# A hybrid mLSTM and attention trunk in split float32: stacked score operands, first loads in another order, a last block in two banks, new order lists

## The chip, the core and the metric

The kernel runs on one core of one Trainium2 chip. The metric is the device time of one execution in microseconds (us). The kernel before was run three times: 927.72, 929.80 and 930.09 us, median 929.80 us. One further execution was profiled.

## What is computed

An encoder trunk of two layers on 256 tokens of width 1024, all in float32. Each layer has a SwiGLU block, a mixer and another SwiGLU block, each followed by a layer norm of the scaled input plus the block's output. The mixer of layer 0 is a bidirectional chunkwise mLSTM with 4 heads, that of layer 1 is windowed attention with 16 query heads, 4 key heads, an ALiBi distance term and a sink logit.

```python
def reference(x, ...):
    for l in range(DEPTH):                                  # 2 layers
        x = layer_norm(ALPHA * x + 0.5 * swiglu(x, ffn_w_in[l, 0], ffn_w_out[l, 0]), ln_g[l, 0], ln_b[l, 0])
        j = l // N_MIXERS
        if l % N_MIXERS == 0:
            y = mlstm_mixer(x, ml_w_in[j], ml_gate_b[j], ml_norm_g[j], ml_w_out[j])
        else:
            y = window_attention(x, at_w_in[j], at_sink[j], at_w_out[j])
        x = layer_norm(ALPHA * x + y, ln_g[l, 1], ln_b[l, 1])
        x = layer_norm(ALPHA * x + 0.5 * swiglu(x, ffn_w_in[l, 1], ffn_w_out[l, 1]), ln_g[l, 2], ln_b[l, 2])
    return x

def swiglu(x, w_in, w_out):                                 # 1024 -> 2 * 2816 -> 1024
    gu = x @ w_in
    return (jax.nn.silu(gu[..., :D_FF]) * gu[..., D_FF:]) @ w_out

# window_attention, the scores of one head (HEAD_DIM = 64)
s = q @ k.T * HEAD_DIM ** -0.5 - slope * dist               # where |t - s| <= 128, else -1e30
m = max(max(s), sink); pe = exp(s - m)
attn = pe / (sum(pe) + exp(sink - m)); o = attn @ v

# mlstm_chunkwise weights all pairs of tokens by running maxima of the gates
```

## The kernel before, in words

**Split operands.** TensorE multiplies in its rounded float32 form (fp32r). To keep float32 accuracy every operand is held as two parts, a high one (`_hi`, the rounded value) and a low one (`_lo`, the rest). One exact product is three matmuls into one PSUM bank: high by high, high by low, low by high (`mm3`). The two parts are made by ScalarE (ACT: the cast that gives the high part) and VectorE (DVE: the subtraction that gives the low part); `split_evac` does both for a PSUM bank.

**Weights.** All weights are streamed from memory in pieces of 512 KB. A piece lands in a raw buffer (`w_raw`, 4 of them, and `s_raw`, 8 more in the SwiGLU stages), ACT writes its `w_hi`, DVE its `w_lo` (each a ring of ten places), and TensorE (PE) uses both. There are 412 such splits. The SwiGLU stages compute part of their first product by a seven-product scheme (`seven`), which adds raw pieces to each other (on DVE, or in the transfer itself on the POOL queue) and multiplies by sums `S1` to `S4` of the transposed input `xT`. `down` adds the second product into four banks that stay open through the stage. `b_mm` is the first block of a SwiGLU stage.

**Start.** The four halves of `x` are fetched on ACT's queue and weight pieces on SP's. PE warms up on transposes of the identity (`warm`), transposes `x` in halves (`to_xT`), and begins with the first weight piece.

**mLSTM.** The running maxima of both directions are in 64 rows. Their high and low parts are two tiles `pn_hir` and `pn_lor` of 128 rows, the rest zero. `weights(h)` spreads one row over 128 partitions by a matmul with a column of the negated identity `neg_id`, once for each part.

**Attention.** Two query heads stand one above the other in 128 rows of `q_hir` and `q_lor` (64 rows each). The keys are in `kp_hir` and `kp_lor`, twice, once in the upper 64 rows with zeros below and once below zeros, so that one matmul of 512 columns gives the scores of both heads (2 x 256 keys). `scores(j)` runs for a pair of heads j (0 to 7) and two token blocks: three such matmuls and one more with `neg_id` that subtracts the distances `dist`. Then follow the maximum (`rm`, DVE), the exponential (`sc`, ACT), the division (`scale`, POOL), eight transposes (`turn`), their split (`pr`), the product with the values (`values`) and the sum of its parts into `q_hir` and `q_lor` of that pair, whose queries are no longer needed. Projections still due (`q_rest`) and output products (`out_proj`) stand between the steps.

**Last norm.** `tail` finishes the four output blocks one after the other; `Norm` takes the statistics of each 512 columns (`half`), then mean, spread, and two passes (`finish`). The result goes out in four transfers.

**Order.** Every instruction is first recorded (`Program`) and then issued in the order of a list of numbers, `ORDER`; another table, `SLOTS`, gives the place of each tile in its ring. Both are written out in the file. Each engine runs its own instructions strictly in that order. Since all operations pass through one recording helper, all have its line in the profile (L301): they are told apart by the names of their tiles.

## Time and profile before

| | |
|---|---|
| median of three runs | 929.80 us (927.72 to 930.09) |
| the profiled execution | 931.54 us, its span 929.8 us |
| mean granted TensorE clock | 0.997 |
| busy: PE, weight loads, DVE, ACT, POOL | 98%, 82%, 87%, 62%, 16% of the span |
| matmuls | 4368 |
| memory read | 206.65 MB |

The profiled execution lasted 1.7 us longer than its span, and 1.7 us longer than the median of the three others. In the profile a matmul is listed with the time from its start to its modelled end. Matmuls overlap, so the time that one costs is the distance between the starts of two that follow each other. `PEld` is the loading of the stationary operand, which overlaps PE. SPq and POOLq are the transfers that SP and POOL start.

### The profile page before, as it was taken

Reading aid. Unit: us, or ns where it says so; the run is one execution under the profiler, and the core shown is the slowest. Engines: PE = TensorE matmul, PEld = TensorE weight load, DVE = VectorE, ACT = ScalarE, POOL = GpSimd, SP = SyncE. Lnnn points to the kernel's source line nnn. Section 1 sums busy time; section 2 is a strip of 40 time slices with the busy share of each in tenths; the row PEclk is TensorE's granted clock in tenths of the full one; section 3 lists DMA queues with packets and bytes.
Section 4 is the critical chain, followed back from the end, with each engine's and each line's share of the span. In section 5 each row is a group of like instructions: output and inputs, shape, how many; then the busy total and the mean of one; then the engine's idle time right before and its main releaser. Section 6 shows DMA issues by size and latency. Waiting matters only on the chain.

```text
span 929.8 us, 12210 instructions
## 1 busy us (share of the span) xinstructions
PE 912.3 (98%) x4368; PEld 758.3 (82%) x4368; DVE 809.7 (87%) x955; ACT 578.5 (62%) x814; POOL 148.1 (16%) x202
## 2 busy tenths in 40 slices
PE   9999999999999999999999999999999999999996
PEld 7887888889988888888888888888887788888875
DVE  6999789887688999879899997998888799987985
ACT  7766477454764667566647674764678568656650
POOL 0331111010110111112012111112335211202100
PEclk9999999999999999999999999999999999999998
DMA  9999799566283889797968988985732378898751
GB/s 339 301 302 263 248 269 226 182 195 218 87 300 109 248 247 246 245 294 206 302 225 206 272 254 242 289 208 185 250 133 68 136 232 252 218 327 212 231 159 45
DMA packets 100637, 208.50 MB, mean 224 GB/s; under 512 B 6848, under 2 KB 21200, under 8 KB 100576
## 3 DMA queue, kind: packets, MB, share of 16 engines
q1 hardware_dynamic: 82368, 173.04, 52.8%
q0 software_dynamic: 17632, 33.64, 21.4%
q10 hardware_dynamic: 576, 1.05, 0.3%
q8 instruction: 34, 0.56, 0.2%
q14 instruction: 27, 0.22, 0.1%
HBM read 206.65 MB, written 1.05 MB: 223 GB/s over the span
## 4 chain that ended last, share of the span: by engine, by line
PE 78%; DVE 7%; DMA 5%; issue 4%; ACT 4%; POOL 0%; SPq 0%; POOLq 0%; ACTq 0%; DVEq 0%
PE p L301 78%; DVE w_lo L301 4%; DMA s_raw<-in_ffn_w_in_dram 3%; ACT w_hi L301 2%; DMA w_raw<-in_ffn_w_out_dram 1%; DVE s_raw L301 1%; DMA w_raw<-in_ffn_w_in_dram 1%; DVE t L301 0%; ACT wt L301 0%; DMA x<-in_x_dram 0%; SPq L301 0%; DVE x L301 0%; DVE pr_lor L301 0%; ACT t L301 0%; DVE rm L301 0%
## 5 line engine op out<-in xcount | busy, mean ns | idle before, releaser
L301 ACT CAST w_hi<-s_raw 128x1024 fp32r<-128x1024 f32 x234 | 240.4, 1051 | 128.8 <-DMA s_raw<-in_ffn_w_in_dram 36.6
L301 DVE TENSOR_TENSOR w_lo<-s_raw,w_hi 128x1024 fp32r<-128x1024 f32 x234 | 278.5, 1218 | 28.7 <-ACT w_hi L301 28.5
L301 DVE TENSOR_TENSOR w_lo<-w_raw,w_hi 128x1024 fp32r<-128x1024 f32 (+1 forms) x171 | 205.2, 1215 | 29.2 <-ACT w_hi L301 28.8
L301 ACT CAST w_hi<-w_raw 128x1024 fp32r<-128x1024 f32 (+1 forms) x171 | 176.9, 1046 | 80.4 <-PE p L301 42.9
L301 PE MATMUL p<-w_hi,xT_hi 128*128 128x512 f32 x512 | 204.3, 399 | 0.0
L301 PE MATMUL p<-w_lo,xT_hi 128*128 128x512 f32 x512 | 199.7, 390 | 1.1 <-DVE w_lo L301 1.1
L301 PE MATMUL p<-w_hi,xT_lo 128*128 128x512 f32 x512 | 200.1, 391 | 0.0
L301 PE MATMUL p<-w_hi,h_hir 128*128 128x512 f32 x320 | 125.6, 393 | 0.0
L301 PE MATMUL p<-w_lo,h_hir 128*128 128x512 f32 x320 | 124.7, 390 | 0.8 <-DVE w_lo L301 0.8
L301 PE MATMUL p<-w_hi,h_lor 128*128 128x512 f32 x320 | 124.9, 390 | 0.4 <-DVE h_lor L301 0.4
L301 PEld LDWEIGHTS p<-w_hi,xT_lo 128*128 128x128 f32 x512 | 96.3, 188 | 20.8
L301 PEld LDWEIGHTS p<-w_lo,xT_hi 128*128 128x128 f32 x512 | 96.5, 188 | 19.9 <-DVE w_lo L301 1.4
L301 PEld LDWEIGHTS p<-w_hi,xT_hi 128*128 128x128 f32 x512 | 96.5, 188 | 19.0 <-ACT w_hi L301 0.4
L301 POOL DMA_DIRECT2D s_raw<-in_ffn_w_in_dram x42 | 51.1, 1218 | 330.1 <-DVE w_raw L301 87.7
L301 PE MATMUL p<-w_hi,S_hir 128*128 128x512 f32 x256 | 100.0, 391 | 1.1 <-ACT t L301 1.1
L301 PE MATMUL p<-w_lo,S_hir 128*128 128x512 f32 x256 | 99.8, 390 | 0.7 <-DVE w_lo L301 0.7
L301 PE MATMUL p<-w_hi,S_lor 128*128 128x512 f32 x256 | 99.7, 389 | 0.0
L301 PEld LDWEIGHTS p<-w_hi,h_lor 128*128 128x128 f32 x320 | 60.1, 188 | 13.7 <-DVE h_lor L301 1.1
L301 PEld LDWEIGHTS p<-w_lo,h_hir 128*128 128x128 f32 x320 | 60.1, 188 | 13.4 <-DVE w_lo L301 1.2
L301 PEld LDWEIGHTS p<-w_hi,h_hir 128*128 128x128 f32 x320 | 60.1, 188 | 12.0
L301 PEld LDWEIGHTS p<-w_hi,S_hir 128*128 128x128 f32 x256 | 48.1, 188 | 12.1 <-ACT t L301 2.2
L301 PEld LDWEIGHTS p<-w_lo,S_hir 128*128 128x128 f32 x256 | 48.1, 188 | 11.0 <-DVE w_lo L301 1.1
(201 smaller groups left out, 1204.6 us busy)
## 6 DMA issues: line engine op xcount, KB each, us to landing
s_raw<-in_ffn_w_in_dram SPq DMA_DIRECT2D x104, 512.0 KB, 6.6
w_raw<-in_ffn_w_in_dram SPq DMA_DIRECT2D x56, 512.0 KB, 5.8
s_raw<-in_ffn_w_out_dram SPq DMA_DIRECT2D x54, 512.0 KB, 6.6
s_raw<-in_ffn_w_in_dram POOLq DMA_DIRECT2D x42, 512.0 KB, 6.7
w_raw<-in_ffn_w_out_dram SPq DMA_DIRECT2D x34, 512.0 KB, 7.1
w_raw<-in_ml_w_in_dram SPq DMA_DIRECT2D x24, 512.0 KB, 4.7
w_raw<-in_ffn_w_in_dram POOLq DMA_DIRECT2D x22, 512.0 KB, 7.6
w_raw<-in_at_w_in_dram SPq DMA_DIRECT2D x12, 512.0 KB, 4.0
```

The source lines that it names most:

```text
L301: f(*args, **kw)
```

## The change

- **Scores from stacked parts.** For each head the high part of the query (64 rows) stands over its low part (64 rows) in one tile `q2r`, and the keys stand twice in `kk_hir` and in `kk_lor`. One matmul of 256 columns with `kk_hir` then adds high by high and low by high, and one with `kk_lor` the other two products. A pair of heads takes four matmuls of 256 columns in place of three of 512. The distance matmul of 512 columns stays and comes first. The queries are split in 64-row pieces (`stacked`), twice as many as before; the keys in 128-row pieces, half as many; the zeroing of `kp` and `pn` on POOL goes.
- **Maxima stacked.** High and low part of the running maxima stand in one tile `pnr`; one matmul with `neg_two`, which has -1 in two rows, replaces two.
- **First loads.** The halves of `x` go on SP's queue among the first weight pieces, the first piece in two transfers, the second piece is split in halves too. The second warm-up has 6 transposes instead of 10. The transposes of the second token block come after that block's first need, those of the second half of the columns one weight piece later.
- **Last columns in two banks.** The last three weight pieces of the last output block are multiplied in two halves of 256 columns, the second half into a bank of its own, and statistics are taken in three parts.
- **Lists anew.** `ORDER` and all of `SLOTS` are new, and attention has two raw buffers more. The new order lets matmuls of several products take turns on PE, where the old one had them mostly in blocks.

```diff
@@ -35,248 +35,267 @@
-WHOLE = 21792
+WHOLE = 21728
...
-    "0 1 1 1 2 35 -34 63 -61 1 75 -74 1 89 -88 1 1 1 1 1 1 156 -155 1 1 22 -19 1 -3 4 1 93 -92 13 -18 6 1 -26 27 "
...
+    "10 -10 9 2 -10 12 1 -12 13 1 -13 14 1 -14 15 1 -15 16 1 -16 17 -16 17 1 -17 18 3 1 1 4 84 -87 1 -6 7 2 116 "
...
@@ -378,7 +397,10 @@
             t = t.rearrange("p (k f) -> p k f", k=w["k"])
-            if isinstance(w["src"], list):
+            if i == 0:
+                for k in range(2):
+                    self.nc.sync.dma_start(t[:, k], w["src"][:, k])
+            elif isinstance(w["src"], list):
                 for k, src in enumerate(w["src"]):
@@ -390,7 +412,7 @@
         lo = self.rooms.take("w_lo", [128, D], FR)
-        if i == 0:
+        if i < 2:
             for j in range(2):
...
@@ -563,16 +583,22 @@
         s_ = slice(h * 512, h * 512 + 512)
-        nc.scalar.dma_start(xt[t][:, s_], x[0, t * 128:(t + 1) * 128, s_])
+        nc.sync.dma_start(xt[t][:, s_], x[0, t * 128:(t + 1) * 128, s_])
 
     xT = (state.tile([128, 8, S], FR, name="xT_hi", tag="xT_hi"),
           state.tile([128, 8, S], FR, name="xT_lo", tag="xT_lo"))
+    for name, n in (("stats", 18), ("mv", 2), ("rs", 2)):
+        rooms.kind(name, tiles(name, n, F32, 2))
 
     W = Weights(nc, rooms, words, plan, after)
     load_x(0, 0)
+    W.load(plan[0]["word"])
     load_x(1, 0)
+    W.load(plan[1]["word"])
     load_x(0, 1)
     load_x(1, 1)
+    W.load(plan[2]["word"])
+    W.load(plan[3]["word"])
     nc.scalar.preload_act_table(AF.Silu)
@@ -600,6 +627,7 @@
         nc.vector.tensor_scalar(neg_id, ident, -1.0, None, op0=OP.mult)
+        nc.vector.scalar_tensor_tensor(neg_two, ident[:, 0:64], -1.0, ident[:, 64:128], op0=OP.mult, op1=OP.subtract)
 
@@ -656,7 +684,15 @@
             self.t, self.ca, self.eps, self.gb, self.last = t, ca, eps, gb, last
-            self.stats = rooms.take("stats", [128, 2, 6], F32)
+            self.stats = rooms.take("stats", [128, 3 if last and t else 2, 6], F32)
+
+        def add(self, c, y, ca=None):
+            z = xt[self.t][:, c:c + 256]
+            nc.vector.scalar_tensor_tensor(z, z, ca or self.ca, y, op0=OP.mult, op1=OP.add)
+
+        def piece(self, i, c, y, ca=None):
+            self.add(c, y, ca)
+            nc.vector.bn_stats(self.stats[:, i], xt[self.t][:, c:c + 256])
 
@@ -685,14 +721,26 @@
                 final = t == 1 and o == 1
+                own = len(todo[t]) - 3 if last and final else None
                 for n, (c, w) in enumerate(todo[t]):
                     if between is not None and t == 0 and o == 1 and n == turn_at:
                         between()
                     if final and n == turn_at:
                         emit_x(0, last)
-                    mm3(y[t][o], h(c, t), pair(w, A, 0, slice(o * 512, o * 512 + 512)),
-                        first and n == 0, n == len(todo[t]) - 1)
-                norm[t].half(o, y[t][o])
+                    if own is not None and n >= own:
+                        mm3(y[t][o][:, 0:256], h(c, t), pair(w, A, 0, slice(512, 768)), False, n == len(todo[t]) - 1)
+                    else:
+                        mm3(y[t][o], h(c, t), pair(w, A, 0, slice(o * 512, o * 512 + 512)),
+                            first and n == 0, n == len(todo[t]) - 1)
+                if own is None:
+                    norm[t].half(o, y[t][o])
+                else:
+                    z = ybank()
+                    norm[t].piece(1, 512, y[t][o][:, 0:256])
+                    norm[t].add(768, y[t][o][:, 256:512])
+                    for n, (c, w) in enumerate(todo[t][own:]):
+                        mm3(z[:, 0:256], h(c, t), pair(w, A, 0, slice(768, 1024)), n == 0, n == 2)
+                    norm[t].piece(2, 768, z[:, 0:256], 1.0)
             norm[t].finish()
@@ -716,8 +764,7 @@
                 to_xT(0, xt[0], ybank, (0,))
-                warm(10)
-                to_xT(1, xt[1], ybank, (0,))
+                warm(6)
             hs, pieces = [], []
@@ -781,10 +828,12 @@
                     for a in range(4):
-                        if m == 0 and a == 1:
+                        if m == 0 and a == 2:
                             for t in range(2):
                                 to_xT(t, xt[t], ybank, (1,))
                         for t in range(2):
+                            if m == a == 0 and t:
+                                to_xT(1, xt[1], ybank, (0,))
                             b_mm(ps[t], t, m, a)
@@ -955,9 +1004,7 @@
                     nc.gpsimd.memset(p[:, :, 256:258].bitcast(F32), one)
-            pn = both([128, S], "pn")
-            for p in pn:
-                nc.gpsimd.memset(p.bitcast(F32), 0.0)
+            pn = tile_([128, S], FR, "pn")
             ones = tile_([64, 1], F32, "ones")
@@ -1006,9 +1053,7 @@
                 nc.vector.tensor_tensor_scan(pm[q, ord_], ones[q].to_broadcast([32, S]), u[q, ord_], 0.0, op0=OP.mult, op1=OP.max)
-            dst = pair(pn, slice(0, 64))
-            nc.scalar.copy(dst[0], pm)
-            nc.vector.tensor_sub(dst[1], pm, dst[0].bitcast(F32))
+            split_evac((pn[0:64], pn[64:128]), pm)
             ex = fe
@@ -1035,9 +1080,7 @@
                     r = 32 * d + h
-                    sel = neg_id[:, r:r + 1].to_broadcast([128, 128])
-                    nc.tensor.matmul(pb[:, d], sel, pn[0], start=True, stop=False)
-                    nc.tensor.matmul(pb[:, d], sel, pn[1], start=False, stop=True)
+                    nc.tensor.matmul(pb[:, d], neg_two[:, r:r + 1].to_broadcast([128, 128]), pn, start=True, stop=True)
                 for sb in range(2):
@@ -1202,9 +1245,7 @@
                 nc.gpsimd.memset(qs_col[64 * (h % 2):64 * (h % 2) + 64, h // 2:h // 2 + 1], 0.125 / slope[8 + h])
-            kp = both([128, 4, 2, S], "kp")
-            for p in kp:
-                nc.gpsimd.memset(p.bitcast(F32), 0.0)
+            kk = both([128, 4, S], "kk")
             fwd = tile_([128, 2, S], F32, "fwd", tag="sc", bufs=6)
@@ -1218,7 +1259,8 @@
             va = [tile_([128, 4, 2, 64], FR, f"v{t}") for t in range(2)]
-            qT = both([128, 8, S], "q")
+            q2 = tile_([128, 8, 2, S], FR, "q2")
+            rooms.kind(f"raw.{keys[bound[0]]}", raws + pool.new("s_raw", D, 2, F32))
             kd, qd = [], []
@@ -1248,15 +1290,19 @@
                     nc.tensor.transpose(p[:, g], kd[t][:, g].rearrange("p a d -> p (a d)"), ident)
-                for a in range(2):
-                    r = slice(64 * a, 64 * a + 64)
-                    split_evac(pair(kp, r, A, a, tok(t)), p[r])
+                split_evac(pair(kk, A, A, tok(t)), p)
+
+            def stacked(j, a, m, src, scale=None):
+
+                r = slice(64 * a, 64 * a + 64)
+                split_evac((q2[0:64, j, a, m], q2[64:128, j, a, m]), src[r], scale[r] if scale is not None else None)
 
             def q_turn(t):
                 p = ybank((128, 4, 128))
                 for j in range(4):
                     nc.tensor.transpose(p[:, j], qd[t][:, j], ident)
-                split_evac(pair(qT, A, slice(0, 4), tok(t)), p)
+                for a in range(2):
+                    stacked(slice(0, 4), a, tok(t), p)
 
@@ -1268,7 +1314,8 @@
                     if k == 7:
-                        split_evac(pair(qT, A, 4 + 2 * g + f), p, qs_col[:, 2 * g + f:2 * g + f + 1])
+                        for a in range(2):
+                            stacked(4 + 2 * g + f, a, A, p, qs_col[:, 2 * g + f:2 * g + f + 1])
                         if f == 1:
@@ -1296,8 +1343,10 @@
                     p = ps[t]
-                    mm3(p, pair(qT, A, j, tok(t)), pair(kp, A, g), True, False)
-                    nc.tensor.matmul(p, neg_id, dist[:, t, None, :].to_broadcast([128, 2, S]), start=False, stop=True)
+                    nc.tensor.matmul(p, neg_id, dist[:, t, None, :].to_broadcast([128, 2, S]), start=True, stop=False)
+                    for a in range(2):
+                        for e in range(2):
+                            nc.tensor.matmul(p[:, a], q2[:, j, a, tok(t)], kk[e][:, g], start=False, stop=a == e == 1)
                     nc.vector.reduce_max(rm[:, t], p, axis=AX.X)
@@ -1391,7 +1440,7 @@
                     o = sums.pop(st - 3)
-                    d = pair(qT, A, st - 3)
+                    d = q2[:, st - 3, 0], q2[:, st - 3, 1]
                     nc.scalar.copy(d[0], o)
@@ -1404,7 +1453,7 @@
             todo = [(c, wo[c]) for c in range(8)]
-            return tail(y, lambda c, t: pair(qT, A, c, tok(t)), (todo[7:], [todo[c] for c in range(8) if c not in CT]), False, norm, last, 4)
+            return tail(y, lambda c, t: (q2[:, c, 0, tok(t)], q2[:, c, 1, tok(t)]), (todo[7:], [todo[c] for c in range(8) if c not in CT]), False, norm, last, 4)
 
```

What the list does to the order is seen in the instructions as they stand on an engine. In the rows below a number behind a name is a buffer.

On PE, in the first SwiGLU stage, the first of the seven products: `S_hir` and `S_lor` are the parts of `S1`, `xT` those of the input, `h` those of the activations for `down`, `p` is a PSUM bank. Before:

```order
L301 MATMUL p_95<-w_hi_71,S_hir_0_159 128x512
L301 MATMUL p_95<-w_lo_81,S_hir_0_159 128x512
L301 MATMUL p_95<-w_hi_71,S_lor_0_160 128x512
L301 MATMUL p_95<-w_hi_71,S_hir_0_159 128x512
L301 MATMUL p_95<-w_lo_81,S_hir_0_159 128x512
L301 MATMUL p_95<-w_hi_71,S_lor_0_160 128x512
L301 MATMUL p_95<-w_hi_73,S_hir_0_159 128x512
L301 MATMUL p_95<-w_lo_82,S_hir_0_159 128x512
L301 MATMUL p_95<-w_hi_73,S_lor_0_160 128x512
```

The same place after:

```order
L320 MATMUL p_91<-w_hi_75,xT_hi 128x512
L320 MATMUL p_92<-w_hi_70,S_hir_0_160 128x512
L320 MATMUL p_92<-w_lo_86,S_hir_0_160 128x512
L320 MATMUL p_91<-w_lo_83,xT_hi 128x512
L320 MATMUL p_94<-w_hi_76,h_hir_1_99 128x512
L320 MATMUL p_91<-w_hi_75,xT_lo 128x512
L320 MATMUL p_92<-w_hi_70,S_lor_0_161 128x512
L320 MATMUL p_94<-w_lo_80,h_hir_1_99 128x512
L320 MATMUL p_91<-w_hi_75,xT_hi 128x512
L320 MATMUL p_92<-w_hi_77,S_hir_0_160 128x512
```

The block of one product has become three products in turn, each with its own pieces of weights.

On PE, in attention, the scores of one token block and what follows them. Before:

```order
L301 MATMUL p_88<-kp_hir_0_230,q_hir_0_241 128x512
L301 MATMUL p_88<-kp_lor_0_231,q_hir_0_241 128x512
L301 MATMUL p_88<-kp_hir_0_230,q_lor_0_242 128x512
L301 MATMUL p_88<-distr_0_238,neg_id 128x512
L301 MATMUL p_94<-xT_hi,w_hi_74 128x256
L301 MATMUL p_94<-xT_lo,w_hi_74 128x256
L301 MATMUL p_94<-xT_hi,w_lo_84 128x256
```

After, the two token blocks of a pair of heads (`p_91` and `p_95`):

```order
L320 MATMUL p_91<-distr_0_238,neg_id 128x512
L320 MATMUL p_94<-xT_lo,w_hi_68 128x256
L320 MATMUL p_91<-kk_hir_0_230,q2r_0_241 128x256
L320 MATMUL p_91<-kk_lor_0_231,q2r_0_241 128x256
L320 MATMUL p_95<-kk_hir_0_230,q2r_0_241 128x256
L320 MATMUL p_91<-kk_hir_0_230,q2r_0_241 128x256
L320 MATMUL p_94<-xT_hi,w_lo_82 128x256
L320 MATMUL p_91<-kk_lor_0_231,q2r_0_241 128x256
```

Each block has five matmuls instead of four, four of them of half the length, and those of the other block and of a projection (`p_94`) stand between them.

On ACT, at the very start. Before:

```order
L301 CAST w_hi_68<-w_raw_64 128x512
L301 CAST xT_hi<-p_89 128x4x128
L301 CAST w_hi_68<-w_raw_64 128x512
L301 ACT_TABLE_LOAD
L301 CAST xT_hi<-p_91 128x4x128
L301 CAST w_hi_69<-w_raw_65 128x1024
```

After:

```order
L320 CAST w_hi_73<-w_raw_64 128x512
L320 CAST xT_hi<-p_95 128x4x128
L320 CAST w_hi_73<-w_raw_64 128x512
L320 CAST w_hi_71<-w_raw_65 128x512 x2
L320 CAST xT_hi<-p_90 128x4x128
L320 CAST w_hi_75<-w_raw_67 128x1024
```

The cast of the second token block's transposed input (`xT_hi<-p_91` before, `xT_hi<-p_90` after) now stands behind both halves of the second weight piece, and the four transfers that ACT issued ahead of all this are gone.

91 lines of the change are left out of this document (45 added, 46 removed), and 397 rows, old and new, of the table ORDER.

## The prediction

> **What bounds the kernel now.** I read the page first, for the engines and the chain.
>
> ```profile
> PE 912.3 (98%) x4368; PEld 758.3 (82%) x4368; DVE 809.7 (87%) x955; ACT 578.5 (62%) x814; POOL 148.1 (16%) x202
> ...
> PE 78%; DVE 7%; DMA 5%; issue 4%; ACT 4%; POOL 0%; SPq 0%; POOLq 0%; ACTq 0%; DVEq 0%
> ```
>
> PE is busy for 912.3 of 929.8 us and carries 78% of the chain that ends last. So PE work that goes away counts almost in full, and so does every wait on PE. DVE, with 87%, is the only other engine that can become the bound. Next I read the waits of PE.
>
> ```profile
> PE p L301 <- DVE w_lo L301: 2.6, 3, 1.1
> PE p L301 <- DVE ident L301: 1.5, 1, 1.5
> PE p L301 <- ACT t L301: 1.1, 2, 0.7
> PE p L301 <- DMA x<-in_x_dram: 0.7, 1, 0.7
> PE p L301 <- ACT q_hir L301: 0.7, 2, 0.4
> PE p L301 <- ACT kp_hir L301: 0.6, 1, 0.6
> PE p L301 <- DVE pr_lor L301: 0.5, 1, 0.5
> PE p L301 <- ACT sc L301: 0.4, 1, 0.4
> PE p L301 <- DVE h_lor L301: 0.4, 1, 0.4
> PE p L301 <- DVE a_lor L301: 0.3, 1, 0.3
> PE p L301 <- POOL sc L301: 0.2, 1, 0.2
> PE p L301 <- DVE kp_lor L301: 0.2, 1, 0.2
> ```
>
> The columns are the time in total, the number of waits and the longest. Without `ident` and `x`, which belong to the start, there are 14 waits that sum to 7.0 us. Seven are attention's (`q_hir`, `kp`, `pr`, `sc`; 2.6 us), three are for weights. The rest of the time PE runs at the pace of its matmuls. That pace, and what a wait costs, I took from the timeline of PE.
>
> ```profile
> 641.01 0.39 PE L301 MATMUL p<-w_lo,h_hir 128*128 128x512 f32 x1
> ...
> 648.04 0.39 PE L301 MATMUL p<-w_hi,h_lor 128*128 128x512 f32 x1
> ```
>
> The first column is the start in us. Between these two rows lie 31 steps of matmuls of 512 columns, so one costs 7.03 / 31 = 0.227 us. The PSUM bank changes after every third of them, and the step does not.
>
> ```profile
> 214.25 0.28 PE L301 MATMUL p<-xT_lo,w_hi 128*128 128x256 f32 x1
> ...
> 219.76 0.28 PE L301 MATMUL p<-xT_hi,w_lo 128*128 128x256 f32 x1
> 219.88 0.28 PE L301 MATMUL p<-pn_hir,neg_id 128*128 128x256 f32 x1
> ...
> 220.33 0.28 PE L301 MATMUL p<-xT_hi,w_hi 128*128 128x256 f32 x1
> ```
>
> From the first to the second row are 46 steps: 0.120 us for 256 columns, a little more than half of 0.227. The four matmuls with `pn` take 0.45 / 4 = 0.113 us each.
>
> ```profile
> 897.57 0.39 PE L301 MATMUL p<-w_hi,S_lor 128*128 128x512 f32 x1
> 898.66 0.50 PE L301 MATMUL p<-w_hi,S_hir 128*128 128x512 f32 x1 [0.71 <-ACT t L301]
> ```
>
> Here a wait of 0.71 us made a step of 1.09 instead of 0.227: it cost 0.86, 0.15 more than it lasted. With that the 14 waits cost 7.0 + 14 x 0.15 = 9.1 us.
>
> **The change part by part.** All sums are made against the profiled execution (931.54 us, span 929.8) and carried over to the median of the three runs, 929.8, as differences.
>
> *Scores.* Eight pairs of heads by two token blocks make 16 blocks. In each, three matmuls of 512 (0.680) become four of 256 (0.480): 0.20 saved, 16 x 0.20 = 3.2 us, all on PE. The saving hangs on the short matmul keeping its 0.120. 46 in a row keep it. The Trainium skill, TensorE: Matmul & The Clock Gate, section Back-to-back issue gap, has another rule: in a sustained stream a matmul takes about 131 ns at 512 columns and 81 at 128. On a straight line between these an estimate for 256 columns is 98 ns, three of 131 cost what four of 98 do, and the term would be 0, the sum of all parts 5.6 us instead of 8.8. The rows above, 227 and 120 ns, disagree with it.
>
> The price is on ACT and DVE: the queries' split takes twice the instructions at half the rows, and an instruction costs by its columns. The two more of 512 columns are given back by the keys; four more of 256 are left on either engine, at 0.42 (worked out with the last block below) 1.7 us, spread over the projections. DVE has 13% free, so I cost it at nothing; uncovered it would be 1.7 us. POOL loses the zeroing of the keys, off every path.
>
> *Maxima.* Eight matmuls at 0.113 go: 0.9 us. `neg_two` is one small DVE instruction more, early, bounded by 0.2.
>
> *Last block.* Nine matmuls of 512 become 18 of 256: 9 x (0.240 - 0.227) = +0.12 us.
>
> ```profile
> 921.31 0.39 PE L301 MATMUL p<-w_hi,h_lor 128*128 128x512 f32 x1
> 921.74 0.69 DVE L301 SCALAR_TENSOR_TENSOR x<-x,p 128x512 f32<-128x512 f32 x1 [0.89 <-PE p L301]
> 922.46 0.69 DVE L301 BATCH_NORM_STATS2 stats<-x 128x6 f32<-128x512 f32 x1
> ```
>
> After the last matmul DVE needs the sum and the statistics of 512 columns, 2 x 0.72 = 1.44 us. For 256 columns I take 0.42 (half would be 0.35, the bounds are 0.35 and 0.69). In the 1.08 us of the last nine matmuls DVE gets through the first 256 columns' sum and statistics and the other sum, 1.3 us, so it is 0.2 to 0.3 late; then 0.42 twice: 1.1 us. Saved 0.32, with PE's 0.12 net 0.2 (0 to 0.5).
>
> *Start.*
>
> ```profile
> 2.00:3.00 1.00, 1.00 (x6) 1.00 (x5) 0.00 (x0) 0.24 (x1) 0.00 (x0) 1.00 0.61 190
> 3.00:4.00 1.00, 0.85 (x4) 0.45 (x3) 0.00 (x0) 1.00 (x1) 0.00 (x0) 1.00 0.92 313
> ```
>
> ```profile
> 4.54 1.12 PE L301 MATMUL p<-ident,x 128*128 128x128 f32 x4 [0.70 <-DMA x<-in_x_dram]
> 5.45 0.62 ACT L301 CAST w_hi<-w_raw 128x512 fp32r<-128x512 f32 x1 [1.41 <-DMA w_raw<-in_ffn_w_in_dram]
> ...
> 8.30 0.78 PE L301 MATMUL p<-w_hi,xT_hi 128*128 128x512 f32 x1
> ...
> 9.72 0.41 PE L301 MATMUL p<-w_hi,xT_hi 128*128 128x512 f32 x1
> ...
> 12.59 0.47 PE L301 MATMUL p<-w_hi,xT_hi 128*128 128x512 f32 x1
> ```
>
> In the first view the last column is GB/s. Before, `x` shares the transfers with the first piece and lands at 4.5; PE begins the first piece at 8.30 and the second at 12.59, with all transposes done; so two pieces are done at 12.59 + 12 x 0.227, with the slow first step 15.4. After, the first half of `x` is alone in front. Its 0.26 MB are through at about 3.2 by the rates above, and I take 3.7 for its landing. Six warm-up transposes and the casts put the first matmul at about 5.9, and the halves of the first `w_lo` hold its six to 7.7; transposes of the second block to 8.1. Then comes the new wait: on ACT the cast of this block's `xT_hi` is queued behind two half casts of the second piece. That piece lands at about 7.4: 1.57 MB stand up to it in the queue, 0.50 are through at 4.0, the rest goes at 313 GB/s. Two half casts of 0.62 and its own 0.59 (0.58 to 0.62 for 512 columns) bring the cast to 9.25, `xT_lo` with DVE's 0.69 to 9.95, and three more matmuls end the first piece at 10.65. The second takes 12 x 0.227 to 13.4, eight transposes to 14.2. The third piece needs the second half of the columns at once, where before a whole piece lay between: about 0.6 lost. That is 14.9 against 15.4: 0.5 saved, between -0.7 (the second piece later by its place in the queue) and 1.3 (no new waits).
>
> On the clock, the three matmuls from 8.30 to 9.72 take 0.47 each, so the slow clock ends within 1.4 us of the first real matmul. The Trainium skill, TensorE: Matmul & The Clock Gate, says under PE-mode transpose (Part 4) that transposes do not engage the full clock, and under The HAM clock gate (Part 1) that it takes some 3.4 us of activity. By that rule the early matmuls would run at half pace for 3.4 us, an estimate of 1.4 us lost, and the sum would be 7.4. The trace, with its 1.4 us, speaks for transposes that count.
>
> *Lists.* They leave the work alone and move the waits: 9.1 us is what they can save, and what they can add is not bounded by the trace. For: with three products in turn, a late `t` or `h_lor` has matmuls of the others between it and its use. Against: a piece of weights stays in use longer. Counted along the order at 0.227 us a step, 2.1 of the ten `w_hi` places are between first and last use on average before, 3.2 after; that leaves DVE a lead of some seven pieces, which is enough. In attention the PE work between a pair's scores and its transposes, counted in the same way, does not get longer: 6.1 to 10.6 us before, 6.2 to 10.8 after; the shortest, the last pair's, had the wait for POOL of 0.2. I take a little over half of the 9.1 as left, 5.1: saved 4.0.
>
> The sum: -3.2 - 0.9 - 0.2 - 0.5 - 4.0 = -8.8 us: 921.0, of which 4.8 is work and 4.0 is waits.
>
> **The rivals.**
>
> *Nearly all waits go* (0.14). Only the three for weights stay, 2.0 us: 929.8 - 4.8 - 7.1 = 917.9. For it: the order can put matmuls of other products in every such place. Against: the transfers' landings, which an order cannot know exactly.
>
> *Only the work goes* (0.17). The waits move but cost the same: 925.0. Attention's seven speak for it, since its chain through DVE, ACT and POOL is as long as before.
>
> *Attention gives its saving back* (0.10). Shorter scores make a pair of heads need less PE time, and the unchanged chain then ends last in every step; the start gives nothing either: -0.9 - 0.2 = -1.1, 928.7. For it: PE already waited at a distance of 6.1 us, and three of the eight pairs now have 6.2 to 6.5. Against: five have over 7.
>
> *Short matmuls in turn with long ones cost more* (0.02). Such turns, one by one, are not in the rows above; if a short one cost 0.17 there, four of them would be 0.68 and the scores would save nothing: 921.0 + 3.2 = 924.2. Against: the step from 256-column projections to `pn` and back keeps its pace. The rule of the Trainium skill in TensorE: Matmul & The Clock Gate, section Back-to-back issue gap, would give the same time.
>
> *Slower: DVE loses its lead* (0.17). Pieces held open longer let ACT and DVE write later, and each time PE comes to a `w_lo` that is not there. One such wait is 1.1 us in the waits above, with 0.15 more. Four SwiGLU stages have four groups of seven products each; if 13 more of these 16 had one, 13 x 1.25 = 16.3 us, 929.8 - 4.8 + 16.3 = 941.3. It decides from six such waits on. For it: DVE's 87% leaves little to catch up with, and the three weight waits that exist are the longest kind. Against: the seven free places.
>
> **How the numbers follow.** The forecast, 921.0, gets 0.40. What a measurement of this kernel can tell from no change is about 0.3%, 2.8 us: below 927.0 is faster, above 932.6 slower. Forecast, both better and work-only cases and the short-matmul case are faster: 0.40 + 0.14 + 0.17 + 0.02 = 0.73. Attention's giving back is the same, 0.10; the loss of DVE's lead slower, 0.17. The range begins at 914: no waits at all (9.1), the start at its 1.3, the last block at its 0.5 make 915.2, and the three runs scatter by 1 us. It ends at 930, above the giving back, and leaves out the slow case.
>
> **What would show it.** Matmuls of 256 columns at 0.120 also where they take turns with those of 512; scores of 16 x 0.20 less on PE; PE's last matmul of the second piece 0.5 earlier; DVE's last sum at 0.42; and in PE's waits a sum near 3.5 us with `w_lo` at no more than 2.6. It is wrong if the waits for `w_lo` have grown by more than 4 us, if PE's busy time falls by less than 3 us, or if the waits for `sc`, `pr` and `q2r` together exceed 5 us.

## The result, and the profile after

| | before | after |
|---|---|---|
| median of 12 runs of each, in turns | 930.30 us (927.70 to 931.69) | 930.83 us (928.30 to 933.29) |
| the profiled execution, its span | 931.54, 929.8 us | 930.4, 928.7 us |
| granted TensorE clock in it | 0.997 | 0.995 |

The ratio is 1.0006, with an interval of 0.9993 to 1.0020: no change. The forecast of 921.0 was wrong, and the result lies outside its range. Before's profiled execution was 1.2 us above its median and after's 0.4 below, so their spans differ by 1.1 us in the other direction; the accounts of single executions below are good to about 1 us. Two executions, of 1303 us (stacked) and 1862 us (before), stand far from all others and are left out of the medians below.

First the page of after, its engines and its chain.

```profile
PE 912.4 (98%) x4381; PEld 749.5 (81%) x4381; DVE 817.4 (88%) x964; ACT 580.5 (63%) x818; POOL 142.6 (15%) x198
...
PE 92%; ACT 3%; DVE 2%; DMA 1%; issue 1%; POOL 0%; SPq 0%; POOLq 0%; ACTq 0%
```

PE carries 92% of the chain instead of 78%, as if nearly all waits had gone, and yet its busy time did not fall (912.3 before). The waits of PE:

```profile
PE p L320 <- ACT xT_hi L320: 2.9, 2, 2.6
PE p L320 <- DVE ident L320: 1.5, 1, 1.5
PE p L320 <- POOL sc L320: 0.9, 1, 0.9
PE p L320 <- DVE w_lo L320: 0.6, 2, 0.4
PE p L320 <- ACT t L320: 0.5, 1, 0.5
PE p L320 <- DVE nm L320: 0.4, 1, 0.4
PE p L320 <- DVE o L320: 0.4, 1, 0.4
PE p L320 <- DVE pr_lor L320: 0.3, 1, 0.3
```

Without the start (`ident`, `xT_hi`) they sum to 3.1 us, where the forecast had 3.5. So the listed waits came out as foreseen, and the time is elsewhere. The view of waits can't say where, because busy time holds slow steps too. I therefore laid an account over the starts of all matmuls: each gets the step that it takes without a wait (512 columns 0.2267, 256 columns 0.120, 128 columns 0.109 us), and whatever a step lasted beyond that is lost time, by stretch of the span. The last column is from the start of the last matmul to the end of the span; the 1.5 us ahead of the first matmul are in no column. Rows other than before and after are of the experiments below.

| profile of | work without waits | lost to 20 us | 20 to 650 | 650 to 750 (attention) | from 750 | end |
|---|---|---|---|---|---|---|
| before | 898.7 | 4.6 | 7.3 | 6.5 | 2.9 | 8.5 |
| before, a second time | 898.7 | 5.1 | 7.7 | 6.1 | 2.9 | 8.5 |
| after | 894.3 | 8.4 | 7.5 | 7.2 | 1.3 | 8.7 |
| xt_first | 894.3 | 6.3 | 7.5 | 7.1 | 1.3 | 8.7 |
| fours | 894.3 | 8.7 | 5.8 | 7.5 | 1.1 | 8.7 |
| spread | 898.7 | 4.4 | 15.3 | 7.2 | 4.0 | 8.5 |
| stacked | 894.5 | 3.4 | 10.8 | 13.1 | 1.9 | 8.5 |
| stacked_pad | 898.1 | 3.6 | 8.5 | 8.6 | 1.9 | 8.5 |
| half_split | 898.7 | 3.9 | 7.6 | 7.8 | 1.8 | 8.5 |
| warm_gap | 896.9 | 4.8 | 9.6 | 7.2 | 1.2 | 8.7 |
| best1 | 894.3 | 6.0 | 5.8 | 7.5 | 1.0 | 7.9 |
| best1_pad | 897.9 | 6.2 | 9.8 | 6.0 | 1.2 | 7.9 |

The work fell by 4.4 us: the 4.0 foreseen for scores, maxima and the last block together, and four warm-up transposes. The start took 3.8 us more, attention 0.7, the end 0.2; only the part from 750 us gave 1.6. From 20 us to the last matmul 16.7 us are lost before and 16.0 after, so of the lists' 4.0 there is 0.7.

The start, in the timeline of after and in its windows (the last three columns are the granted clock, the DMA share and GB/s):

```profile
1.45 2.39 PE L320 MATMUL p<-ident 128*128 128x128 f32 x10 [1.45 <-DVE ident L320]
...
4.49 0.95 PE L320 MATMUL p<-ident 128*128 128x128 f32 x6
5.38 0.51 PE L320 MATMUL p<-w_hi,xT_hi 128*128 128x512 f32 x1
...
7.76 0.60 PE L320 MATMUL p<-ident,x 128*128 128x128 f32 x4
9.32 1.14 ACT L320 CAST w_hi<-w_raw 128x512 fp32r<-128x512 f32 x2 [2.91 <-DMA w_raw<-in_ffn_w_in_dram]
10.37 0.58 ACT L320 CAST xT_hi<-p 128x512 fp32r<-128x512 f32 x1
11.00 0.50 PE L320 MATMUL p<-w_hi,xT_hi 128*128 128x512 f32 x1 [2.64 <-ACT xT_hi L320]
...
12.43 0.63 PE L320 MATMUL p<-w_hi,xT_hi 128*128 128x512 f32 x1
12.86 0.63 PE L320 MATMUL p<-w_lo,xT_hi 128*128 128x512 f32 x1
...
18.34 0.50 PE L320 MATMUL p<-w_hi,xT_hi 128*128 128x512 f32 x1 [0.24 <-ACT xT_hi L320]
```

```profile
0.00:2.00 2.00, 0.55 (x3) 0.55 (x4) 0.23 (x1) 1.21 (x1) 0.42 (x5) 1.00 0.08 15
2.00:4.00 2.00, 2.00 (x11) 1.97 (x10) 0.00 (x0) 0.07 (x1) 0.00 (x0) 1.00 0.93 307
4.00:6.00 2.00, 2.00 (x12) 1.58 (x10) 1.16 (x2) 1.34 (x3) 0.00 (x0) 1.00 0.79 235
6.00:8.00 2.00, 1.70 (x8) 1.05 (x8) 0.83 (x2) 0.41 (x1) 0.00 (x0) 1.00 0.87 292
...
10.00:12.00 2.00, 0.91 (x3) 0.46 (x3) 1.51 (x3) 0.94 (x2) 0.00 (x0) 0.90 1.05 400
12.00:14.00 2.00, 2.00 (x5) 1.61 (x6) 0.80 (x2) 1.97 (x3) 0.00 (x0) 0.50 1.05 387
14.00:16.00 2.00, 2.00 (x8) 1.54 (x8) 2.00 (x3) 1.56 (x2) 0.00 (x0) 0.75 1.05 388
```

PE waits 2.64 us for the cast of the second token block, which stands behind two half casts of a piece that lands at 9.3. Then the granted clock is halved for (0.10 + 0.50 + 0.25) x 2 / 0.5 = 3.4 us, up to 15.0: the nine steps from 11.00 to 14.99 take 3.99 us, where nine of 0.227 take 2.04; without the 0.15 that a restart costs, this is 1.8 us more. From 12.43 on each takes 0.43. They count as busy, which is a part of why PE's busy time hid the saved work. The third piece begins at 18.34, not at 14.9; before it began at 15.43.

The clock's first rise comes at another moment in every profile. In after it is at 4.75 us: the transposes ahead of it start 0.21 us apart, those behind it 0.11 (the view of windows prints 1.00 also ahead of the first record of the clock). In the six profiles with the old start (before twice, spread, stacked, stacked_pad, half_split) it comes between 6.9 and 10.6 us, and the later it comes, the more is lost to 20 us, 3.4 to 5.1. So the 3.8 is good to about 1 us, and after's loss is not owed to a late rise.

The end, in the timelines, first DVE of after, then the last transfers of before, after and the best version below:

```profile
919.88 0.42 DVE L320 BATCH_NORM_STATS2 stats<-x 128x6 f32<-128x256 f32 x1
920.29 0.42 DVE L320 SCALAR_TENSOR_TENSOR x<-x,p 128x256 f32<-128x256 f32 x1
...
924.19 0.75 DVE L320 SCALAR_TENSOR_TENSOR x<-x,rs,w_raw 128x512 f32<-128x512 f32 x1
```

```profile
919.55 7.70 SPq L301 DMA_DIRECT2D out_dram<-x  x4
```

```profile
917.07 8.23 SPq L320 DMA_DIRECT2D out_dram<-x  x4
```

```profile
913.76 7.63 SPq L312 DMA_DIRECT2D out_dram<-x  x3
```

The sum of 256 columns takes 0.42, and the path from the last matmul to DVE's last write is 0.6 us shorter. But from the end of the last issue (927.25 before, 925.30 after) to the end of the span (929.8 and 928.7) it is 3.4 us after against 2.6 before: 0.8 given back.

### The profile page after: what moved, and what is told of

Same layout as the page of the kernel before. It is cut to its first block, busy times and chain, and to the rows that moved or that the text cites. A ratio compares the mean times of both kernels' runs of the same rounds, so it can differ in the third digit from the quotient of the medians.

```text
span 928.7 us, 12294 instructions
## 1 busy us (share of the span) xinstructions
PE 912.4 (98%) x4381; PEld 749.5 (81%) x4381; DVE 817.4 (88%) x964; ACT 580.5 (63%) x818; POOL 142.6 (15%) x198
## 4 chain that ended last, share of the span: by engine, by line
PE 92%; ACT 3%; DVE 2%; DMA 1%; issue 1%; POOL 0%; SPq 0%; POOLq 0%; ACTq 0%
PE p L320 92%; ACT w_hi L320 1%; ACT sc L320 1%; DMA w_raw<-in_ffn_w_in_dram 1%; DMA s_raw<-in_ffn_w_out_dram 1%; DVE pr_lor L320 0%; DVE w_lo L320 0%; DVE x L320 0%; ACT q2r L320 0%; DVE rm L320 0%; DVE o L320 0%; DVE s_raw L320 0%; POOL sm L320 0%; ACT es L320 0%; POOL sc L320 0%
## 5 line engine op out<-in xcount | busy, mean ns | idle before, releaser
L320 ACT CAST w_hi<-s_raw 128x1024 fp32r<-128x1024 f32 x246 | 253.4, 1052 | 101.7 <-PE p L320 62.4
L320 DVE TENSOR_TENSOR w_lo<-s_raw,w_hi 128x1024 fp32r<-128x1024 f32 x246 | 293.8, 1220 | 20.5 <-ACT w_hi L320 15.5
L320 DVE TENSOR_TENSOR w_lo<-w_raw,w_hi 128x1024 fp32r<-128x1024 f32 (+1 forms) x160 | 191.5, 1213 | 30.2 <-ACT w_hi L320 26.5
L320 ACT CAST w_hi<-w_raw 128x1024 fp32r<-128x1024 f32 (+1 forms) x160 | 164.5, 1040 | 78.6 <-PE p L320 35.6
L320 PE MATMUL p<-w_hi,xT_hi 128*128 128x512 f32 x512 | 198.8, 402 | 2.9 <-ACT xT_hi L320 2.9
L320 PE MATMUL p<-w_lo,h_hir 128*128 128x512 f32 (+1 forms) x323 | 120.9, 393 | 0.0
L320 PE MATMUL p<-w_hi,h_hir 128*128 128x512 f32 (+1 forms) x323 | 120.7, 393 | 0.0
L320 PE MATMUL p<-w_hi,h_lor 128*128 128x512 f32 (+1 forms) x323 | 119.7, 393 | 0.0
L320 PE MATMUL p<-w_hi,S_hir 128*128 128x512 f32 x256 | 96.6, 392 | 0.5 <-ACT t L320 0.5
L320 PEld LDWEIGHTS p<-w_lo,h_hir 128*128 128x128 f32 x323 | 60.6, 188 | 13.1 <-DVE w_lo L320 0.3
L320 ACT CAST h_hir<-p 128x512 fp32r<-128x512 f32 x40 | 23.4, 585 | 56.9 <-PE p L320 56.7
```

Of the source, the lines that this page charges most:

```text
L320: f(*args, **kw)
```

## The experiments

Two places of the loss were in sight, the start and the pace; where the lists' gain had gone was not. Each kernel runs beside the kernel before on the same chip, whose median was 930.0 to 931.0. The lists of after were not run without the rest of the change; what they are worth is worked out from differences below.

**xt_first**: after, with the second block's casts ahead of the second piece's; on ACT (on DVE the same with `xT_lo` and `w_lo`):

```diff
 CAST xT_hi<-p_95 128x4x128
 CAST w_hi_73<-w_raw_64 128x512
+CAST xT_hi<-p_90 128x4x128
 CAST w_hi_71<-w_raw_65 128x512 x2
-CAST xT_hi<-p_90 128x4x128
```

> The kernel after, with one edit at the start: on ACT the cast of xT_hi of the second token block, and on DVE its difference xT_lo, come ahead of the two half casts of the second piece of weights. Theory (the start lost it): in the profile of after PE waits 2.64 us for this cast, until 11.00, because the two half casts ahead of it wait for a piece that lands at 9.3; and after that idle time the granted clock is 0.50 from 11.58 to 14.99, where nine steps take 0.43 instead of 0.227 us. With the cast in front PE starts again at about 9.0, the idle time is under 1 us, the clock stays at 1.00, and 2.0 + 1.8 us, less some 0.3 of new waiting for the second piece, go: 3.5 us less than after, 927.3. Rival 1 (only the landing counts): the wait moves on to the second piece's own casts, the clock falls all the same, and under 1 us is gained: 930. Rival 2 (the fall of the clock has nothing to do with idle PE): the wait goes, the slow steps stay, 2.0 us: 928.8.

Measured: 928.55 us (12 runs), ratio 0.9979 (0.9969 to 0.9990); 2.3 below after.

```profile
9.51 0.50 PE L315 MATMUL p<-w_hi,xT_hi 128*128 128x512 f32 x1 [0.68 <-ACT xT_hi L315]
...
16.22 0.50 PE L315 MATMUL p<-w_hi,xT_hi 128*128 128x512 f32 x1 [1.15 <-ACT xT_hi L315]
```

```profile
12.00:14.00 2.00, 2.00 (x10) 1.60 (x9) 0.99 (x1) 2.00 (x3) 0.00 (x0) 1.00 1.05 386
```

The wait shrinks from 2.64 to 0.68, and the clock stays at 1.00: in that window stand ten matmuls instead of five. Over whole executions the mean clock was 0.997 or more in all 12, where after had it in 3 of 12 (928.3, 928.6 and 929.1 us; the other nine have a median of 931.2). A wait of 1.15 for the second half's cast is left. So the start cost after some 2.3 us by this one order of casts, wait and clock together, where 3.5 had been expected. The time alone would fit the second rival (928.8, the slow steps stay) as well; the clock in the trace, and in all 12 executions, speaks against it.

**warm_gap**: to part the clock from the wait, after with 24 transposes of the identity in PE's idle time, behind those of the second block:

```diff
                                 to_xT(1, xt[1], ybank, (0,))
+                                for j in range(24):
+                                    nc.tensor.transpose(ps[1].rearrange("p (k m) -> p k m", k=4)[:, j % 4], ident, ident)
```

> The kernel after with one edit at the start: 24 transposes of the identity, 24 x 0.107 = 2.6 us of work that nothing uses, stand on PE between the transposes of the second token block and its first matmul, where PE is idle for 2.6 us in the profile of after; no wait is made shorter by it. Theory (the idle time itself lowers the granted clock, and transposes count as work): the clock stays at 1.00, the nine steps of 0.43 us become 0.227, and 1.8 to 2.5 us go although PE has more to do: 928.3 to 929.0, every execution's mean clock at 0.997 or more. Rival (transposes don't count as work for the clock): 0.50 from about 11.6 to 15.0 as before, 930.8 or a little more, most executions at 0.995 or 0.996.

Measured: 931.18 us (12 runs), ratio 0.9997 (0.9980 to 1.0013).

```profile
8.93 2.78 PE L315 MATMUL p<-ident 128*128 128x128 f32 x24
11.47 0.49 PE L315 MATMUL p<-w_hi,xT_hi 128*128 128x512 f32 x1
...
13.36 0.40 PE L315 MATMUL p<-w_hi,xT_hi 128*128 128x512 f32 x1
13.59 0.39 PE L315 MATMUL p<-w_lo,xT_hi 128*128 128x512 f32 x1
13.82 0.39 PE L315 MATMUL p<-w_hi,xT_lo 128*128 128x512 f32 x1
```

The steps are 0.23 where after had 0.43, and 9 of 12 executions had a clock of 0.997 or more, against 3 of 12: with the idle time filled the clock mostly stays. It had been expected to stay in all; in three it was 0.996. The time was not better, though, where 928.3 to 929.0 had been expected. In its profile the start with the added transposes is 1.0 us shorter than after's (4.8 + 2.6 against 8.4), and 20 to 650 us lose 2.1 us more, which is not explained.

What the half clock costs can be estimated within each kernel. The median of the executions with a clock under 0.997 lies above that of the others by 2.6 us in after (9 and 3 executions), by 2.2 in fours below (9 and 3) and by 2.7 in warm_gap (3 and 9); the slow steps of the one profile come to 1.8. And the three of after that kept the clock have a median of 928.56, that of xt_first. By these few executions most of the 2.3 us is the clock's, and the shorter wait is worth little.

**fours** and **spread**: the pace. Where four transposes of a bank stand one by one between matmuls of 512 columns, each might cost more. fours is after with them gathered at the place of the last (239 groups become 88); spread is before with 69 of its groups of four pulled apart (73 become 280). A place of fours on PE, then one of spread:

```diff
-MATMUL p_93<-ident,t_2_156 128x128
 MATMUL p_91<-w_lo_82,xT_hi 128x512
 MATMUL p_90<-w_lo_86,h_hir_1_99 128x512
 MATMUL p_95<-w_hi_73,xT_hi 128x512
-MATMUL p_93<-ident,t_2_156 128x128
 MATMUL p_89<-w_hi_75,h_lor_0_100 128x512
 MATMUL p_95<-w_lo_85,xT_hi 128x512
-MATMUL p_93<-ident,t_2_156 128x128
 MATMUL p_95<-w_hi_73,xT_lo 128x512
-MATMUL p_93<-ident,t_2_156 128x128
+MATMUL p_93<-ident,t_2_156 128x128 x4
```

```diff
+MATMUL p_94<-ident,t_3_156 128x128
 MATMUL p_92<-w_hi_76,h_hir_0_104 128x512
+MATMUL p_94<-ident,t_3_156 128x128
 MATMUL p_92<-w_lo_80,h_hir_0_104 128x512
+MATMUL p_94<-ident,t_3_156 128x128
 MATMUL p_92<-w_hi_76,h_lor_0_106 128x512
-MATMUL p_94<-ident,t_3_156 128x128 x4
+MATMUL p_94<-ident,t_3_156 128x128
```

> The kernel after, with one edit in the list: where the four transposes of a bank stand among other products' matmuls, they stand together again, at the place of the last of them (239 groups of transposes behind the start become 88); nothing else moves. Theory (taking turns has a price): in the two traces a transpose alone between matmuls of 512 columns adds 0.140 us, four together 0.455, eight 0.882, so each change from matmuls to transposes and back costs about 0.03 us. 151 changes fewer give 151 x 0.028 = 4.2 us, if the waits stay: 926.6. Rival (a transpose costs 0.11 wherever it stands, and the lists gained less than they seem to): nothing in the pace changes and the later transposes add a wait or two: 931 to 932.

> The kernel before, with one edit in the list: of 69 of its groups of four transposes each transpose is put between two of the matmuls that stood ahead of them or behind them (75 groups become 282); nothing else moves. Theory (taking turns has a price): 207 changes more at 0.0275 us are 5.7 us, with some waits for transposes that now end later: 936 (935 to 938). Rival (no price): 930.3, at most 0.7 more from such waits.

Measured: fours 928.8 us (12 runs), ratio 0.9987 (0.9971 to 1.0003), 2.0 below after (the two intervals overlap; its profile loses 1.7 less between 20 and 650 us); spread 941.17 (5 runs), ratio 1.0107 (1.0088 to 1.0125). The price of one is read in the timeline of PE, for a group of four in before and a lone one in after:

```profile
314.20 0.39 PE L301 MATMUL p<-w_lo,xT_hi 128*128 128x512 f32 x1
...
314.66 0.60 PE L301 MATMUL p<-ident,t 128*128 128x128 f32 x4
...
315.56 0.40 PE L301 MATMUL p<-w_hi,xT_lo 128*128 128x512 f32 x1
```

```profile
356.78 0.40 PE L320 MATMUL p<-w_hi,h_hir 128*128 128x512 f32 x1
...
357.25 0.27 PE L320 MATMUL p<-ident,t 128*128 128x128 f32 x1
...
357.82 0.40 PE L320 MATMUL p<-w_hi,xT_hi 128*128 128x512 f32 x1
```

From 314.20 to 315.56 stand four matmuls of 512 and four transposes: (1.36 - 4 x 0.227) / 4 = 0.113 us a transpose. From 356.78 to 357.82 four matmuls and one transpose: 1.04 - 0.91 = 0.13. Over all places without a wait a lone one between matmuls of 512 costs 0.12. Over all of them the mean transpose costs 0.1138 us in before, 0.1193 in after, 0.1129 in fours and 0.1236 in spread. With 356 of them the turns of after cost 356 x 0.0055 = 2.0 us, which is what fours gained, half of what was expected: the price of a lone one was set too high. In spread they cost 3.5 us of some 11. Of the other 7 its list of waits shows 4.8 (14.0 us in 22 waits, before 9.2 in 16), most of them for `t`, the input of the transposes, many of which stand earlier than before. As a measure of the price spread is spoiled.

**stacked** and **half_split**: before with one part each. stacked takes the scores from stacked parts and the stacked maxima into the old list; half_split takes only the finer split of the later queries, four instructions more on ACT and on DVE.

```diff
-                    mm3(p, pair(qT, A, j, tok(t)), pair(kp, A, g), True, False)
-                    nc.tensor.matmul(p, neg_id, dist[:, t, None, :].to_broadcast([128, 2, S]), start=False, stop=True)
+                    nc.tensor.matmul(p, neg_id, dist[:, t, None, :].to_broadcast([128, 2, S]), start=True, stop=False)
+                    for a in range(2):
+                        for e in range(2):
+                            nc.tensor.matmul(p[:, a], q2[:, j, a, tok(t)], kk[e][:, g], start=False, stop=a == e == 1)
```

```diff
-                        split_evac(pair(qT, A, 4 + 2 * g + f), p, qs_col[:, 2 * g + f:2 * g + f + 1])
+                        for a in range(2):
+                            r = slice(64 * a, 64 * a + 64)
+                            split_evac(pair(qT, r, 4 + 2 * g + f), p[r], qs_col[r, 2 * g + f:2 * g + f + 1])
```

> The kernel before with its own loads, its own last block and its own list; only the stacked scores and the stacked maxima are taken over, their operations standing where the old ones stood. Theory (the work that goes is time that goes): 3.2 us for 64 matmuls of 256 columns instead of 48 of 512, 0.9 for eight matmuls fewer: 4.1 us less than before, 926.2. Rival (attention gives it back, its chain through DVE, ACT and POOL being as long as ever): only the 0.9 of the maxima, 929.4, and PE's waits in attention grow by some 3 us. A second rival (short matmuls among long ones cost 0.17): 929.4 too, but with steps of 0.17 in the trace.

> The kernel before with one edit: the split of the later heads' queries is made in two halves of 64 rows, as the stacked form needs it, so that ACT and DVE have four instructions of 256 columns more each; the scores stay as they were. Theory 1 (cover) expects no more than these instructions' own delay where PE waits for the queries: 930.3 to 931.3. Theory 2 (the stacked form's instructions lengthen attention's chain): most of what stacked lost is here, 933 to 934.5.

Measured: stacked 934.26 us (11 runs), ratio 1.0038 (1.0025 to 1.0051); half_split 932.75 (12 runs), ratio 1.0025 (1.0011 to 1.0038). The saving by itself made the kernel 3.9 us slower, against 926.2 in the theory and 929.4 in its rivals; half_split, 2.7 slower, lies just below the range of the second theory. PE's waits in attention, 660 to 745 us of stacked:

```profile
PE p L297 <- DVE pr_lor L297: 2.3, 4, 0.9
PE p L297 <- POOL sc L297: 1.7, 3, 1.0
PE p L297 <- ACT sc L297: 1.4, 2, 0.9
PE p L297 <- DVE q2r L297: 1.4, 3, 0.8
PE p L297 <- ACT q2r L297: 0.7, 2, 0.4
PE p L297 <- DVE sc L297: 0.2, 1, 0.2
```

They come to 7.7 us in 15 waits, all for a pair's queries, scores, probabilities and sums; in the same stretch before has 2.6 us in 7, half_split 3.4 in 9. By the account the work is 4.2 less than before and attention loses 6.6 more. The stretch from 20 to 650 us, where this edit changes nothing but the small work of the maxima, also loses 3.5 more in this profile, 1.9 of it in the list of waits (4.8 against 2.9 us); why, isn't explained (with the pad below it is 1.2). The finer split has a price of its own: 2.7 us by the medians, of which its profile shows 1.3 in attention. Where the rest stands is open: the profiled execution, 931.41, was 1.3 us below the median.

**stacked_pad**: is it the PE work that covered the chain? stacked with 16 matmuls more that do nothing, one ahead of each block's scores (16 x 0.227 = 3.6 us of work):

```diff
                     p = ps[t]
+                    nc.tensor.matmul(p, neg_id, dist[:, t, None, :].to_broadcast([128, 2, S]), start=True, stop=True)
                     nc.tensor.matmul(p, neg_id, dist[:, t, None, :].to_broadcast([128, 2, S]), start=True, stop=False)
```

> The kernel stacked with one matmul more in each of its 16 score blocks: the distance matmul of 512 columns is issued twice, the second starting the sum anew, so that 16 x 0.227 = 3.6 us of PE work are added and no other engine has anything more to do. In stacked (934.5) PE's waits in attention, at the queries, the probabilities and the scaled exponentials, grew by 6.3 us while 3.2 us of PE work went. Theory 1 (cover: the chain of a pair of heads through DVE, ACT and POOL lasts as long as before, and the matmuls that went were what PE did meanwhile): the added work fills waits, and the time stays within 1 us of stacked: 934 to 935.5. Theory 2 (the stacked form lengthens the chain itself, by its four more split instructions on ACT and on DVE and their place ahead of every score): the waits stay and the work comes on top: 937.5 to 938.5.

Measured: 932.87 us (12 runs), ratio 1.0029 (1.0014 to 1.0043).

```profile
PE p L297 <- POOL sc L297: 1.2, 3, 0.5
PE p L297 <- ACT sc L297: 0.7, 2, 0.4
PE p L297 <- ACT q2r L297: 0.7, 2, 0.4
PE p L297 <- DVE pr_lor L297: 0.7, 2, 0.5
PE p L297 <- DVE q2r L297: 0.5, 2, 0.3
```

3.6 us of useless work cost nothing (2.8 us above the kernel before at its side, stacked 3.9): the waits fall from 7.7 to 3.8, and attention loses 4.5 less in the account. The time is below the range of the first theory and far from that of the second. With the pad PE has 0.6 us less work than before, and the 2.8 that are left agree with the 2.7 of the finer split. In the old list the chain through DVE, ACT and POOL sets the time of attention, and PE's saving there can only become waiting.

**before_again**: before, profiled once more, for what of the waits recurs.

> The kernel before, unchanged, for a second profile: which of PE's waits stand in both, and which belong to one execution. Theory: the waits of attention stand in both within 0.2 us each; the single waits for weights (at 74.4, 91.0, 882.9) hang on the landing of transfers and need not. Rival: all of them stand in both, and the profile shown of before is a fair measure of what the list could save.

Measured: 931.92 us, span 930.2. Attention's waits recur, at 6.1 us lost against 6.5. Of the others many move: the longest is now 1.5 us on `h_lor` at 836.7, where the first profile has none, and `w_lo` has 0.9 instead of 2.6. What a list has to work against is in good part chance; its sum was nearly the same in these two profiles (16.7 us lost from 20 us on, and 16.7).

**best1** and **best1_pad**: best1 joins what helped, xt_first and fours, puts the second half's `xT` casts ahead of one later weight cast, and sends the first block's output in one transfer. best1_pad is best1 with the 16 useless matmuls.

```diff
-                if self.last:
+                if self.last and self.t:
                     nc.sync.dma_start(out[0, tok(self.t), s_], z[:, s_])
+            if self.last and not self.t:
+                nc.sync.dma_start(out[0, tok(self.t), :], z)
```

> The kernel after with four edits of its list: xT_first and fours as tried; on ACT and DVE the casts and differences of the second half of x ahead of the cast of a later piece (in xT_first PE still waits 1.15 us for them at 16.2) and ahead of the first Strassen sum; and the first block's output in one transfer instead of two, so that the last output takes the last of the eight semaphores that the end waits for, as in before (in the trace of before 0.9 us lie between the last landing and the end, in that of after 1.7). If the causes add up: 930.8 - 2.3 - 1.0 - 2.0 - 0.8 = 924.7. Rival (they overlap: what one saves another wait takes back): 926.5 to 928, no better than the better of the two edits alone by more than 1.5 us.

> The kernel best1 with the distance matmul of each of its 16 score blocks issued twice, 16 x 0.227 = 3.6 us more on PE and nothing more elsewhere, as in stacked_pad. In the old list the same addition made the time no longer (934.5 before it, 932.9 with it), since it filled waits. Theory 1 (the new list gives PE other work to do in a pair's chain, so PE is what limits attention there): 2.5 to 3.6 us come on top, 928.5 to 929.6. Theory 2 (attention is limited by its chain in the new list as well, and the stacked form is worth little there): at most 1 us, 926 to 927.

Measured: best1 925.97 us (7 runs), ratio 0.9954 (0.9937 to 0.9971), below both kernels and between the theory (924.7) and the rival (926.5 to 928); best1_pad 928.62 (12 runs), ratio 0.9979 (0.9965 to 0.9994). Here the useless work costs 2.65 us by the medians, 1.7 if each is taken against the kernel before at its side, and the two intervals overlap a little. The account of attention says the same: with the pad it loses 1.5 us less (4.5 less in the old list), so that 2.1 of the 3.6 us come on top. (The profile of best1_pad is of the slowest of its 12 executions, with 4.0 us more lost between 20 and 650 us, so only attention is compared.) So in the new list PE sets attention's pace for the larger part: the list pays for the shorter scores by covering the chain with other products. And from the end of the last issue to the end of the span (921.39 to 924.0) it is 2.6 us again. All profiles of the new list with four output transfers have 8.7 us from the last matmul to the end, both with three have 7.9; one transfer is worth 0.8. The records of the last instructions show why. SP waits for the last transfers on each semaphore one after the other, in a fixed order. In before and in best1 the last output's semaphore is the last in that order; the others are passed while it is under way, and from its landing to the end it is 0.9 us (928.92 to 929.83, 923.07 to 923.99). In after the last output's semaphore is one of the first, seven more waits stand behind it (926.99 to 927.82), and it is 1.7 us (926.97 to 928.69).

## Why the prediction was wrong, point by point

In span the forecast was -8.8 us and the profile of after has -1.1. By the account 3.9 of the 7.7 between them are the start's, 3.3 the lists', 0.5 the end's, and nothing is the work's. The two steps that failed most are "0.5 saved" at the start and, of the lists, "they leave the work alone and move the waits".

- *Scores and maxima, -4.1: right as work, wrong as time.* The matmuls of 256 columns take 0.1195 us also in turns with those of 512 (0.126 where a single one stands between two, 11 places), and the work fell by 4.4 in all. The rule of the Trainium skill, TensorE: Matmul & The Clock Gate, section Back-to-back issue gap, by which, in the estimate on a straight line, four of 256 columns cost what three of 512 do, does not hold here: 0.120 and 0.227. But the step "PE carries the chain, so PE work that goes away counts almost in full" failed for attention. In the old list this saving costs 3.9 us (stacked) instead of giving 4.1, and the pad of 3.6 us is free there. "Attention gives its saving back" had 0.10. It came true in the old list, and was bought off by the new one, in which attention loses 0.7 us more than before.
- *Extra split instructions, nothing: wrong.* half_split puts 2.7 us on the four on either engine that were counted. DVE's free 13% is an average over the span; in attention, where its profile shows 1.3 of the 2.7, the split stands in the chain that PE waits for.
- *Lists, -4.0: right on the waits (3.1 left, 3.5 forecast), wrong on the sum.* With 0.15 for each, the waits from 20 us on fell from 9.1 us to 3.8 (2.9 in 6), more than forecast; the steps without a wait gave 4.6 back. 2.0 of these are transposes in turns, a cost that I did not look for. Steps of 512 columns in direct succession were also a little longer, 0.2281 against 0.2275, some 1.5 us in 3000; I found no cause for that. Set against stacked instead of before, the new list with the new start and end takes 934.3 to 930.8 by the medians; with the start's loss of some 3 us set apart it is worth 6 to 7 there, of which 3.9 repay what stacked had lost.
- *Start, -0.5: wrong by 3.9, the largest single term.* It measured +3.4 (3.8 lost, less four warm-up transposes); by the sum's own mark, the start of the third piece, +2.9 (18.34 against 15.43). Between the first matmul and the third piece all was in the sum but two things. The second piece lands at 9.3, not 7.4: by the windows 2 x (15 + 307 + 235 + 292) = 1.70 MB had moved by 8.0 us, more than the 1.57 that stood up to it, so transfers issued later had taken a share. And after the idle time the clock is halved for 3.4 us. The Trainium skill has both halves of this in TensorE: Matmul & The Clock Gate: a window of about 3.4 us by which the clock is set (The HAM clock gate, Part 1), with which the drop of 3.4 us agrees; and, under Why this matters for your kernels, no idle gaps over about 3 us. Here 2.64 us of waiting were enough in most executions. I used the page for the rise only and not for the fall.
- *Transposes count for the clock: right.* In after the clock rose at 4.75 us, when PE had done nothing but transposes (its first product is at 5.38), and warm_gap holds the pace with 24 of them; the same page's PE-mode transpose (Part 4) says that they do not count, and the steps of 0.23 speak against it.
- *Last block, -0.2: right up to DVE (0.42 for the sum, 0.6 us less path), then undone* by 0.8 from the last transfer to the end, the order of SP's last waits, which no step looked at.
- *Rivals.* DVE did not lose its lead: `w_lo` has 0.6 us of waits. Short matmuls in turn cost nothing more; it was the transposes in turn that did.
- *Two slips in the sums.* The terms of the range's lower end give 914.8, not 915.2. The three waits for weights, put at 2.0 us in the case that nearly all waits go, are 2.6 us in their row and 3.0 with 0.15 each, which makes that case 919.0 instead of 917.9. Neither bears on the result.

Of the tests I had named, "PE busy falls by less than 3 us" told the failure at once, though for another reason than meant: the half clock and the lone transposes count as busy.

## What to carry to other kernels

Before counting a saving on the busiest engine, ask stretch by stretch what else would then end last, and test it by adding useless work there: if that is free, so was the work you mean to remove. A re-ordered list brings its own costs (inputs queued behind a late transfer, an idle gap that halves the clock, short operations alone between long ones), and busy time hides the last two; the distance between starts shows them. Here taking out those costs made 0.46% (0.29 to 0.63) of a change that by itself gave nothing.

## What was not expected of the hardware

- A lone transpose of 128 columns between matmuls of 512 costs 0.12 us, one in a group of four 0.113; taking turns made 2.0 us over this kernel.
- A PE that had been idle for 2.64 us had 0.50 of its clock for 3.4 us from 0.6 us after its return on; by the mean clock this came in 9 of 12 executions.
- Transposes alone raise the clock: in after it rose at 4.75 us, ahead of the first product.
- Transfers issued later on a queue take a share before an earlier one has landed: the second piece came 1.3 us or more after its bytes were due.
- The end of the kernel waits for its transfers in a fixed order of semaphores: 0.9 us follow the last landing if the last output's is the last of them, 1.7 if it is one of the first. One transfer fewer decided it here.
